# Opening stage in a fixed block order, operands padded to 512 bytes, and 512-column units in the output and last down projections

## The chip, the cores and the metric

The kernel runs on one core of one Trainium2 chip. A core has TensorE (matrix products; PE in the profile, PEld for its weight loads), VectorE (DVE), ScalarE (ACT), GpSimd (POOL) and SyncE (SP, which here only issues DMAs). Each engine works through its own instructions in the order of the program and waits on semaphores for the others. The metric is the device time of one launch in microseconds.

## The reference

A trunk of two layers (`DEPTH = 2`) over 512 latent and 256 context tokens of width 1024, all in fp32. Cut to what matters here:

```
shift, scale, gate  = ada_w, ada_b applied to c (latent) or c_ctx (context)   # per layer
h  = modulate(rms_norm(x), shift, scale)
p  = h @ w_in                       # q, k, v, gMLP, conv and gate columns
m  = gated sum of attention(p) @ w_attn_o, gMLP(p) @ w_gmlp_o, conv(p) @ w_conv_o
x  = x + gate * rms_norm(m @ w_out)                    # output projection
h2 = modulate(rms_norm(x), ...)
x  = x + gate * rms_norm(relu(h2 @ w_ff1) ** 2 @ w_ff2)  # w_ff2: down projection, 4096 -> 1024
```

Layer 0 works on all 768 tokens, layer 1 (the last) on the 512 latent tokens, since only those are put out.

## The kernel before, in words

**Three products for one.** Each operand of a large matrix product is split into a high part that TensorE reads at its fast fp32 rate and the remainder. ScalarE casts the high part (`hi`), VectorE or GpSimd subtracts it (`lo`), and TensorE adds hi·hi, hi·lo and lo·hi into the same sums. `wload` (L165 to L175) does this for a 512 KB block of weights: a DMA into `wraw` or `xraw`, the cast to `whi` (L171), the subtraction to `wlo` (L174). `hT` and `hB` are the split activations, stored with the features on the partitions; `split` (L178, L179) makes them.

**Stages.** A start stage (load and normalise the tokens, compute shift and scale of layer 0), then for each layer attention, gMLP, convolution and feed-forward. Tokens go in tiles of 128 and in groups of two tiles: (0,2), (2,2) and, in layer 0, the context group (4,2). A scheduler that simulates a timeline fixes each engine's order; the code order of the Python text is only its input. Buffers are rings by tag (`whi` and `wlo` four each).

**`natural`** (L460) computes the output projection `w_out` of both layers and the last quarter (`ch == 3`) of the down projection. The activations are the stationary operand, 128 tokens at a time, and the weights stream past in 256 columns, so the 1024 output columns make four units. Unit 0 is done jointly for all groups where `joint` is 1; after that each group runs through its remaining units alone and loads the weights of each unit again. After a unit a `sink` squares and scales the 256 columns, and after a group's last unit `after` runs `post_norm` (sum of squares, reciprocal root, X update at L452) and `pre_norm` (normalise, eight transposes per tile on TensorE at L403, modulate, split) for what follows.

**The opening.** Six token tiles X, the ten small parameter loads, 4 blocks j of shift and scale weights (2 MiB of `ada_w` each, L303, multiplied at L310) and the k and v weights (2 MiB) all come through the DMA queue of SyncE. Normalised tokens are transposed (L403), copied to `xT` (L1066, L1068), modulated when block j's shift and scale are there (L1076), and split into `hT`. `keys_values` in the attention stage (L532) then makes k and v in 144 matmuls of 512 columns, k block by k block over all six token tiles. The q projection follows (L206, 256 columns).

**Where operands lie.** Counted modulo 512 bytes in a partition of the core's memory, the program puts `hT`, `whi` and `wlo` at 256, `hB` at 0, `z` at 64, `attn`, `kT` and `qT` at 320, `gin` at 224.

Of the kernel before, what the change touches and what calls it, by code (L numbers as in the profile page):

```python
# [19 lines left out]
P = 128  # L20
D = 1024
KB = D // P
# [18 lines left out]
JOINT_DOWN = [1, 0]  # L41
# [13 lines left out]
def trunk_kernel(ctx: ExitStack, tc: tile.TileContext, x, c, ctx_in, c_ctx, ada_w, ada_b, mix_pre_g, mix_post_g,  # L55
# [4 lines left out]
    cst = ctx.enter_context(tc.tile_pool(name="cst", bufs=1))  # L60
    outer = ctx.enter_context(tc.tile_pool(name="outer", bufs=1))
# [33 lines left out]

    def o_(shape, tag, bufs, dt=F32):
        return outer.tile(shape, dt, tag=tag, bufs=bufs, name=nm(tag))

    def t_(shape, tag, bufs, dt=F32):
        return stage_pool[0].tile(shape, dt, tag=tag, bufs=bufs, name=nm(tag))  # L100

    ident = cst.tile([P, P], F32, name="ident")
# [8 lines left out]
    for r in range(2):  # L111
        nc.gpsimd.memset(pick[:, r, r:r + 1], 1.0)

# [4 lines left out]
    def here(engine):  # L118

        prev = next((i for i in reversed(nc.cur_bb.bb.instructions) if i.engine == engine), None)  # L120
        if prev is None:
            yield
        else:
            with tc.issue_after(prev):
                yield

# [84 lines left out]
    def wload_kv(l, pool_lo, tiles=range(4)):  # L211
        return [wload(w_in[l][k * 256:(k + 1) * 256, K0:K0 + 512], 2, 512, pool_lo) for k in tiles]

# [42 lines left out]
    def parameters():  # L256
        rows = t_([P, 2, P], "rows", 1)
        nc.sync.dma_start(rows[0:96, 1, :], ada_b.rearrange("l (t p) -> (l t) p", p=P))
        yield
        for i, src in enumerate((mix_pre_g, mix_post_g, gmlp_norm_g, conv_b, conv_norm_g, conv_norm_b,  # L260
                                 ffn_pre_g, ffn_post_g)):
            nc.sync.dma_start(rows[16 * i:16 * i + 16, 0, :], src.rearrange("l (t p) -> (l t) p", p=P))
            if i < 6:
                yield
# [4 lines left out]
        nc.tensor.transpose(pv[:, 0:P], rows[:, 0, :], ident)  # L269
        nc.tensor.transpose(pv[:, P:P + 100], rows[0:100, 1, :], ident[:100, :100])  # L270
# [25 lines left out]
    def ada_shift_scale(j):  # L296
# [10 lines left out]
        for v in range(2):  # L307
            for h in range(2):
                for q in range(4):
                    nc.tensor.matmul(pa[32 * q:32 * q + 32, v * 256:(v + 1) * 256], c2[:, 4 * h + q, :],  # L310
                                     raws[2 * v + h][:, q, :], start=h == 0, stop=h == 1, tile_position=(0, 32 * q))
        rows = t_([P, 512], "adrow", 2)
        nc.scalar.copy(rows, pa)
        pt = ps1()
# [3 lines left out]
        nc.vector.tensor_reduce(m, pt.rearrange("p (v t q s) -> p v t s q", v=2, t=2, q=4)[:, :, :, 0:2, :],  # L318
                                axis=AX.X, op=ALU.add)
        ab = vecs[0]["adab"][:, 0:16].rearrange("p (v k) -> p v k", v=2)[:, :, 2 * j:2 * j + 2]  # L320
        for r in range(2):
            nc.vector.tensor_tensor(m[:, :, :, r], m[:, :, :, r], ab, ALU.add)
        for r in range(2):
            nc.vector.scalar_tensor_tensor(m[:, 1, :, r], m[:, 1, :, r], 1.0, vecs[0]["pre"][:, 2 * j:2 * j + 2],
                                           op0=ALU.add, op1=ALU.mult)
# [74 lines left out]
    def transposed(xn, grp, ps, kb):  # L400
        i0, n, _ = grp
        for i in range(n):
            nc.tensor.transpose(ps[:, i * P:(i + 1) * P], xn[i0 + i][:, kb * P:(kb + 1) * P], ident)  # L403
# [56 lines left out]
    def natural(src, xs, parts, joint, sink, after=None, pool_lo=False):  # L460


        def unit(u, some, after=None):
            ws = wload_n(src[:, u * 256:(u + 1) * 256], pool_lo and u > 2)
            for grp in some:
                i0, n, _ = grp
                ps = ps2()
                for i in range(n):
                    gemm_n(ps[:, i * 256:(i + 1) * 256], (i0 + i) * P, ws, xs)
                sink(grp, u, ps[:, :n * 256].rearrange("p (i c) -> p i c", c=256))  # L470
                if after is not None:
# [790 lines left out]
```

## Time and profile before

| | |
|---|---|
| time, median of 3 runs | 2648.12 us (2647.98 to 2650.31) |
| profiled execution, own time | 2647.3 us |
| its span in the profile | 2645.5 us |
| TensorE busy | 2591.1 us (98%), 15133 matmul records |
| VectorE busy | 1658.5 us (63%) |
| ScalarE busy | 1076.2 us (41%) |
| data moved by DMA | 300.13 MB, mean 113 GB/s |

The span goes from the first to the last instruction; the 1.8 us between it and the execution's own time lie outside. The records of matmuls overlap: one lasts longer than the distance to the next one's start, so what a matmul costs is read from the distance between starts, not from its own duration.

### The profile page before, as it was taken

To read this page: it belongs to the slowest core of one execution; us is meant where nothing else is said; L and a number is where in the kernel's file an instruction comes from. 1 tells how busy PE (TensorE), PEld (TensorE's weight loads), DVE (VectorE), ACT (ScalarE), POOL (GpSimd) and SP (SyncE) were. 2 spreads that over 40 slices of the span, in tenths; PEclk is the share of its full clock that TensorE was granted. 3 is DMA by queue.
4 is the path that set the end of the run, shared out by engine and by line. 5 is a ranking of instruction groups with operands and counts; after the bars stand their busy time and mean duration, and the time that the engine had idled before them with its cause. 6 is when DMAs were issued, how large, how long until landed. Compare 5 with 4: busy or idle time off the path is not lost.

```text
span 2645.5 us, 37736 instructions
## 1 busy us (share of the span) xinstructions
PE 2591.1 (98%) x15133; PEld 2266.0 (86%) x15133; DVE 1658.5 (63%) x2663; ACT 1076.2 (41%) x1848; POOL 435.0 (16%) x310
## 2 busy tenths in 40 slices
PE   7999999999999999999999999999999999999998
PEld 5989988888888899888888899888888888988888
DVE  5746847489864648445564478777679855734436
ACT  4646434344134636322131355554343244633324
POOL 0000015466463200000000000000465510000000
PEclk9999999999999999999999999999999999999999
DMA  7211134233345345243464342112433455533233
GB/s 250 63 43 37 36 107 137 62 99 95 104 130 173 102 165 154 76 130 120 127 199 129 121 151 88 57 41 72 124 108 100 138 159 173 155 112 96 96 101 106
DMA packets 322241, 300.13 MB, mean 113 GB/s; under 512 B 11517, under 2 KB 268817, under 8 KB 322065
## 3 DMA queue, kind: packets, MB, share of 16 engines
q1 hardware_dynamic: 309360, 271.20, 33.2%
q10 hardware_dynamic: 12704, 26.51, 2.8%
q8 instruction: 119, 1.95, 0.3%
q14 instruction: 58, 0.47, 0.1%
HBM read 275.63 MB, written 22.04 MB: 113 GB/s over the span
## 4 chain that ended last, share of the span: by engine, by line
PE 92%; DVE 3%; DMA 2%; ACT 2%; issue 1%; SPq 0%; DVEq 0%; ACTq 0%
PE ps L192 44%; PE ps L494 16%; PE ps L206 9%; PE pq L192 8%; PE pq L206 4%; PE pq L669 3%; PE ps L635 2%; PE ps L658 1%; PE ps L532 1%; DVE wlo L174 1%; ACT whi L171 1%; PE ps L919 1%; PE pq L403 0%; PE ps L574 0%; DMA xraw<-in_ada_w_dram 0%
## 5 line engine op out<-in xcount | busy, mean ns | idle before, releaser
L192 PE MATMUL ps<-hB,whi 128*128 128x512 f32 (+1 forms) x2272 | 591.9, 359 | 5.0 <-DVE ff L1175 2.3
L171 ACT CAST whi<-wraw 128x1024 fp32r<-128x1024 f32 x261 | 273.8, 1050 | 638.8 <-PE ps L192 315.9
L174 POOL TENSOR_TENSOR wlo<-wraw,whi 128x1024 fp32r<-128x1024 f32 x96 | 230.7, 2404 | 1549.2 <-ACT whi L171 1533.5
L192 PEld LDWEIGHTS ps<-hB,whi 128*128 128x128 f32 x2272 | 387.6, 188 | 71.3 <-DVE ff L1175 2.7
L837 DVE SCALAR_TENSOR_TENSOR cy<-G,cw,cy 128x768 f32<-128x768 f32 (+1 forms) x464 | 404.3, 888 | 11.5
L192 PE MATMUL ps<-hB,wlo 128*128 128x512 f32 (+1 forms) x1136 | 371.9, 357 | 0.0
L494 PE MATMUL ps<-whi,hT 128*128 128x512 f32 x1152 | 356.7, 389 | 0.6 <-ACT whi L171 0.6
L174 DVE TENSOR_TENSOR wlo<-wraw,whi 128x1024 fp32r<-128x1024 f32 x165 | 204.7, 1241 | 201.1 <-ACT whi L171 196.8
L192 PE MATMUL ps<-hT,whi 128*128 128x512 f32 (+1 forms) x1408 | 318.7, 344 | 0.6 <-ACT gu L915 0.6
L494 PEld LDWEIGHTS ps<-whi,hT 128*128 128x128 f32 x1152 | 216.2, 188 | 46.4 <-ACT whi L171 1.1
L192 PEld LDWEIGHTS ps<-hT,whi 128*128 128x128 f32 x1408 | 221.1, 189 | 34.3 <-ACT gu L915 1.1
L174 DVE TENSOR_TENSOR wlo<-xraw,whi 128x1024 fp32r<-128x1024 f32 x109 | 133.3, 1223 | 185.0 <-ACT whi L171 184.5
L206 PE MATMUL ps<-whi,hT 128*128 128x256 f32 x1280 | 232.0, 283 | 0.0
L192 PEld LDWEIGHTS ps<-hB,wlo 128*128 128x128 f32 x1136 | 199.4, 188 | 31.6
L494 PE MATMUL ps<-wlo,hT 128*128 128x512 f32 x576 | 224.4, 390 | 0.0
L171 ACT CAST whi<-xraw 128x1024 fp32r<-128x1024 f32 x109 | 114.2, 1049 | 258.9 <-PE ps L494 118.9
L206 PEld LDWEIGHTS ps<-whi,hT 128*128 128x128 f32 x1280 | 199.6, 192 | 0.5 <-issue 0.4
L192 PE MATMUL ps<-hT,wlo 128*128 128x512 f32 x704 | 190.2, 343 | 0.0
L206 PE MATMUL ps<-wlo,hT 128*128 128x256 f32 x640 | 181.2, 284 | 0.6 <-DVE wlo L174 0.6
L343 POOL TENSOR_TENSOR asum<-asum,aprod 128x512 f32<-128x512 f32 x84 | 111.6, 1329 | 105.7 <-ACT aprod L341 63.2
L494 PEld LDWEIGHTS ps<-wlo,hT 128*128 128x128 f32 x576 | 108.1, 188 | 22.6 <-issue 0.4
L192 PEld LDWEIGHTS ps<-hT,wlo 128*128 128x128 f32 x704 | 110.2, 189 | 16.0
(299 smaller groups left out, 4315.1 us busy)
## 6 DMA issues: line engine op xcount, KB each, us to landing
wraw<-in_w_in_dram SPq DMA_DIRECT2D x134, 512.0 KB, 3.7
xraw<-in_w_ff_dram SPq DMA_DIRECT2D x89, 512.0 KB, 3.9
wraw<-in_w_ff_dram SPq DMA_DIRECT2D x63, 512.0 KB, 3.9
xraw<-in_ada_w_dram SPq DMA_DIRECT2D x39, 512.0 KB, 5.2
wraw<-in_ada_w_dram SPq DMA_DIRECT2D x33, 512.0 KB, 4.2
araw<-in_ada_w_dram SPq DMA_DIRECT2D x48, 256.0 KB, 2.9
xraw<-in_w_out_dram SPq DMA_DIRECT2D x18, 512.0 KB, 8.3
wraw<-in_w_attn_o_dram SPq DMA_DIRECT2D x16, 512.0 KB, 3.5
```

The costliest lines, as they stand in the source:

```text
L171: nc.scalar.copy(hi, raw)
L174: e.tensor_tensor(lo, raw, hi.bitcast(F32), ALU.subtract)
L192: nc.tensor.matmul(ps[:, d0:d0 + n], wt[:, k, c0:c0 + P], xt[:, s0:s0 + n], start=k == 0 and j == 0, stop=k == nk - 1 and j == 2)
L206: nc.tensor.matmul(o, xt[:, tok0:tok0 + P], wt, start=k == 0 and j == 0, stop=k == nk - 1 and j == 2)
L343: nc.gpsimd.tensor_tensor(sums[r], sums[r], t, ALU.add)
L494: nc.tensor.matmul(o, xt[:, tok], wt[:, k, :], start=kt == k == j == 0, stop=kt == 3 and k == 1 and j == 2)
L532: nc.tensor.matmul(o, xt[:, tok], wt, start=k == 0 and j == 0, stop=k == KB - 1 and j == 2)
L635: nc.tensor.matmul(ps[:, s0 - key0:s0 - key0 + n], a[:, i * P:(i + 1) * P], b[:, s0:s0 + n], start=m == 0, stop=m == 2)
L658: nc.tensor.transpose(pt[:, kt * P:(kt + 1) * P], Pm[:, kt * P:(kt + 1) * P], ident)
L669: nc.tensor.matmul(po[:, :256], a[:, kt0 + kt, vs], b[:, kt, :], start=kt == 0 and m == 0, stop=kt == nkt - 1 and m == 2)
L837: nc.vector.scalar_tensor_tensor(done if t == TAPS - 1 else y, G[:, :, t:t + 256], cw[:, t * 8 + cidx:t * 8 + cidx + 1], y, op0=ALU.mult, ...
L919: nc.tensor.matmul(ps[:, n * P:(n + 1) * P], gv[cidx // 4][:, n, (cidx % 4) * P:(cidx % 4 + 1) * P], wsT[:, g, :], start=True, stop=True)
```

## The change: what it does

1. **`natural` in two units.** The four units of 256 columns become two of 512, each over all groups; four weight blocks of 256 rows by 512 columns per unit. The output and last down projections together go from 1920 matmuls of 256 columns to 960 of 512, and from 70 weight blocks to 32. Sinks work on 512 columns, and `after` of every group comes in unit 1.
2. **The opening in a fixed order.** X tiles first, then `ada_w` and k/v weights block by block; the k and v matmuls move into the start stage (new L1109), interleaved with the blocks, and TensorE's instructions there are kept in the order in which they are written. The four transposes and the reduction behind each shift and scale block become four matmuls with two moving columns (new L342) and two VectorE operations. The bias load goes to ScalarE's queue, and `xraw` has ten buffers instead of six there.
3. **Padding.** Tiles of 512 bytes or more are padded to multiples of 512, smaller ones go to a pool `tiny`. In the program all operands of matmuls then lie at the same place modulo 512 bytes, 192. Three tags are merged or cut (`gb`, `junkg`, and `dg` from `NT` buffers to 2).

```diff
 def natural(...)
-            ws = wload_n(src[:, u * 256:(u + 1) * 256], pool_lo and u > 2)
-            for grp in some:
...
-                    gemm_n(ps[:, i * 256:(i + 1) * 256], (i0 + i) * P, ws, xs)
...
-        for u in range(joint):
-            unit(u, [grp for part in parts for grp in part])
-        for part in parts:
-            for u in range(joint, 4):
-                unit(u, part, after if u == 3 else None)
+        for u in range(2):
+            ws = [wload(src[kt * 256:(kt + 1) * 256, u * 512:(u + 1) * 512], 2, 512, pool_lo and u == 1)
+                  for kt in range(4)]
+            for grp in groups:
+                i0, n, _ = grp
+                ps = ps2()
+                for k in range(KB):
+                    xhi, xlo = xs[k]
+                    whi, wlo = (w[:, k % 2, :] for w in ws[k // 2])
+                    for i in range(n):
+                        tok = slice((i0 + i) * P, (i0 + i + 1) * P)
+                        for j, (xt, wt) in enumerate(((xhi, whi), (xhi, wlo), (xlo, whi))):
+                            nc.tensor.matmul(ps[:, i * 512:(i + 1) * 512], xt[:, tok], wt,
+                                             start=k == 0 and j == 0, stop=k == KB - 1 and j == 2)
+                sink(grp, u, ps[:, :n * 512].rearrange("p (i c) -> p i c", c=512))
+                if u == 1:
+                    after(grp)
             pump(1)
```

```diff
+    def tile_in(pool, shape, tag, bufs, dt, align=LINE):
+
+        size = 2 if dt == BF16 else 4
+        n = math.prod(shape[1:])
+        whole = -(-n * size // align) * align // size
+        if whole == n:
+            return pool.tile(shape, dt, tag=tag, bufs=bufs, name=nm(tag))
+        t = pool.tile([shape[0], whole], dt, tag=tag, bufs=bufs, name=nm(tag))[:, :n]
...
+    nc.gpsimd.memset(tiny.tile([P, FILL], F32, name="fill"), 0.0)
...
         for t in range(4):
-            nc.tensor.transpose(pt[:, t * P:(t + 1) * P], rows[:, t * P:(t + 1) * P], ident)
+            pe(nc.tensor.matmul(pt[:, 2 * t:2 * t + 2], rows[:, t * P:(t + 1) * P], every, start=True, stop=True))
...
-                dg = t_([P, P], "dg", NT)
+                dg = t_([P, P], "dg", 2)
...
+        in_order[0] = True
...
         for j in range(4):
+            ks = (2 * j, 2 * j + 1)
             if j < 3:
                 next(ada[j + 1])
-            next(ada[j])
-            for grp in (LAT, CTXG):
-                for k in (2 * j, 2 * j + 1):
-                    modulated(grp, k)
+                raws.append(kv_raw(j + 1))
+            w_kv.append(kv_parts(raws[j]))
+            for k in ks:
+                modulated(LAT, k)
+            if j:
+                for k in ks:
+                    modulated(CTXG, k)
+            kv_step(LAT, ks[0])
...
+            if j:
+                kv_step(CTXG, ks[0])
+            kv_step(CTXG, ks[1])
+        in_order[0] = False
```

ScalarE's order in the opening, before. `CAST whi` are the weight casts of k/v blocks, `COPY adrow` takes a block's shift and scale out of the sums, `CAST hT` makes the high part of a feature block of the activations.

```order
L313 COPY adrow_344<-pq_327 128x512
L171 CAST whi_252<-xraw_250 128x1024
L171 CAST whi_258<-xraw_256 128x1024
L1068 COPY xT_78_294<-ps_285 128x256
L178 CAST hT_112<-xT_53_207 128x512
L178 CAST hT_114<-xT_54_209 128x512
...
L313 COPY adrow_393<-pq_376 128x512
L178 CAST hT_116<-xT_56_220 128x512
```

The last two k/v weight casts (`whi_252`, `whi_258`) stand ahead of the first `hT` cast. After the change ScalarE has, from the third k/v block's cast (`whi_540`) on:

```order
L206 CAST whi_540<-xraw_450 128x1024
L206 CAST hT_119<-xT_87_367 128x256
L1081 COPY xT_93_385<-pq_380 128x256
L206 CAST hT_121<-xT_88_369 128x256
L1081 COPY xT_96_394<-pq_389 128x256
L338 COPY adrow_421<-pq_404 128x512
L206 CAST whi_618<-xraw_538 128x1024
L206 CAST hT_123<-xT_58_240 128x512
L206 CAST hT_125<-xT_59_242 128x512
```

`whi_618`, the cast of the fourth and last k/v block, now stands between block 1's shift and scale (`adrow_421`) and block 1's first activations (`hT_123`).

TensorE's order at the end of layer 1's output projection, before: `ps_21197` is the last unit of the second group, 48 matmuls, and `Y_20615`, `Y_20616` are the first group's normalised tiles, transposed for the feed-forward.

```order
L206 MATMUL ps_21197<-whi_21193,hT_20481 128x256
L403 MATMUL pq_20999<-ident,Y_20615 128x128
L403 MATMUL pq_21012<-ident,Y_20615 128x128
L206 MATMUL ps_21197<-wlo_21195,hT_20481 128x256
L206 MATMUL ps_21197<-whi_21193,hT_20482 128x256
```

Two of the sixteen transposes of the first feature blocks stand among the unit's last matmuls. And after the change, where `ps_20141` is the second group's second unit:

```order
L497 MATMUL ps_20141<-wlo_20001,hT_19798 128x512
L497 MATMUL ps_20141<-whi_19999,hT_19799 128x512
L426 MATMUL pq_20089<-ident,Y_19815 128x128
L426 MATMUL pq_20102<-ident,Y_19815 128x128
L426 MATMUL pq_20089<-ident,Y_19816 128x128
L426 MATMUL pq_20089<-ident,Y_19815 128x128
```

The first group's transposes stood behind 133 matmuls of the second group (two whole units and 37 of the third's 48); now they stand behind 48, all of its second unit.

## Rows read from the trace of the kernel before

**Rows 1.** The page: busy time of the engines, and the span in 40 slices (tenths)

```profile
PE 2591.1 (98%) x15133; PEld 2266.0 (86%) x15133; DVE 1658.5 (63%) x2663; ACT 1076.2 (41%) x1848; POOL 435.0 (16%) x310
...
PE   7999999999999999999999999999999999999998
...
PEclk9999999999999999999999999999999999999999
```

**Rows 2.** Chain that ended last, runs of matmuls: start us, us, what

```profile
70.45 17.27 PE pq L206 x144
...
635.60 83.67 PE ps L192 x480
...
825.65 41.61 PE ps L192 x240
...
887.73 67.75 PE ps L192 x384
...
2173.13 56.47 PE ps L192 x247
...
2373.50 43.52 PE ps L192 x192
```

**Rows 3.** TensorE's matmuls by line and shape: busy us, mean ns | idle before

```profile
L206 PE MATMUL ps<-whi,hT 128*128 128x256 f32 x1280 | 232.0, 283 | 0.0
...
L206 PE MATMUL ps<-wlo,hT 128*128 128x256 f32 x640 | 181.2, 284 | 0.6 <-DVE wlo L174 0.6
...
L961 PE MATMUL ps<-dg,means 128*128 128x128 f32 x20 | 2.7, 274 | 0.0
```

**Rows 4.** Windows: stretch, us, busy us of each engine, PEclk, DMA share, GB/s

```profile
20.00:30.00 10.00, 7.77 (x79) 4.27 (x78) 9.39 (x28) 5.09 (x8) 0.00 (x0) 1.00 1.08 391
30.00:40.00 10.00, 9.74 (x56) 7.04 (x54) 3.54 (x9) 2.46 (x7) 0.00 (x0) 1.00 1.09 382
40.00:45.00 5.00, 4.95 (x46) 3.19 (x45) 4.11 (x13) 2.23 (x5) 0.00 (x0) 1.00 0.60 172
...
615.00:635.00 20.00, 14.71 (x85) 12.31 (x85) 17.51 (x23) 10.24 (x13) 14.33 (x13) 0.83 0.28 89
```

**Rows 5.** Timeline of the opening: start us, us, engine, line, operation [idle before]

```profile
23.18 0.69 DVE L1066 COPY xT<-ps 128x512 f32<-128x512 f32 x1
...
25.87 1.05 ACT L171 CAST whi<-xraw 128x1024 fp32r<-128x1024 f32 x1 [0.17 <-DMA xraw<-in_w_in_dram]
...
28.04 0.62 ACT L178 CAST hT<-xT 128x512 fp32r<-128x512 f32 x1 [0.85 <-DVE xT L1076]
...
28.71 0.50 PE L532 MATMUL ps<-whi,hT 128*128 128x512 f32 x1 [0.73 <-ACT hT L178]
...
40.08 1.93 PE L310 MATMUL pq<-xraw,c 128*32 128x256 f32 x32
...
70.29 0.28 PE L206 MATMUL pq<-whi,hT 128*128 128x256 f32 x1
```

**Rows 6.** Chain: 48 matmuls before and 48 after an idle stretch

```profile
581.15 8.33 PE ps L192 x48
...
624.21 10.04 PE ps L192 x48
```

**Rows 7.** Timeline, end of layer 1's output projection, group 0's chain

```profile
2259.36 0.38 ACT L1145 ACTIVATE junk<-ps 128x256 bf16<-128x256 f32 x1 [0.45 <-PE ps L206]
...
2271.60 1.41 DVE L398 TENSOR_SCALAR Y<-X,rs 128x1024 f32<-128x1024 f32 x2
...
2275.06 0.38 PE L403 MATMUL pq<-ident,Y 128*128 128x128 f32 x2
```

**Rows 8.** Timeline, layer 0's last down projection, and the kernel's end

```profile
1597.68 0.41 PE L403 MATMUL pq<-ident,Y 128*128 128x128 f32 x2 [1.15 <-DVE Y L398]
...
2636.89 0.28 PE L206 MATMUL ps<-whi,hT 128*128 128x256 f32 x1
...
2638.79 0.63 DVE L1216 TENSOR_TENSOR Y<-Y,Gb 128x256 f32<-128x256 f32 x1 [1.16 <-ACT junk L1145]
```

More of the change, by code (lines that the diff above doesn't have):

```diff
@@ L40 @@
 UP_AHEAD = 6
-JOINT_DOWN = [1, 0]
+LINE = 512
+FILL = 24
 EPS = 1e-6
@@ L498, in streamed, with attention @@
                 tick(kt)
-    def attention(l, hT, T, last, md, w_kv=None):
+    def attention(l, hT, T, last, md, kv_ps=None):
         NT = T // P
@@ L520, in rope_tabs, with keys_values @@
             return C, S
-        def keys_values(ws):
-            pss = [ps2() for _ in range(3)]
-            for k in range(KB):
-                xhi, xlo = hT[k]
-                whi, wlo = (w[:, k % 2, :] for w in ws[k // 2])
-                for i in range(6):
-                    o = pss[i // 2][:, (i % 2) * 512:(i % 2) * 512 + 512]
-                    tok = slice(i * P, (i + 1) * P)
-                    for j, (xt, wt) in enumerate(((xhi, whi), (xhi, wlo), (xlo, whi))):
-                        nc.tensor.matmul(o, xt[:, tok], wt, start=k == 0 and j == 0, stop=k == KB - 1 and j == 2)
+        def keys_values(pss):
             k_nat = t_([P, 6, 256], "PT", 4)
@@ L1043, in x_load @@
             queue.dma_start(t, src)
-    with stage("start", 6):
+    with stage("start", 10):
         conditioning()
@@ L1051, in trunk_kernel, with x_columns @@
         xT = {}
[L1053 to L1055 removed]
+        def x_columns(grp, kbs):
             w = grp[1] * P
[L1057 to L1059 removed]
+            new, per = (ps2, 1024 // w) if grp == LAT else (ps1, 512 // w)
+            for kb in range(kbs[0], kbs[1], per):
+                ps = new()
                 for q in range(per):
@@ new lines, in kv_step @@
+        def kv_step(grp, k):
+            xhi, xlo = hT[k]
+            whi, wlo = (w[:, k % 2, :] for w in w_kv[k // 2])
+            for i in range(grp[0], grp[0] + grp[1]):
+                o = kv_ps[i // 2][:, (i % 2) * 512:(i % 2) * 512 + 512]
+                tok = slice(i * P, (i + 1) * P)
+                for n, (xt, wt) in enumerate(((xhi, whi), (xhi, wlo), (xlo, whi))):
+                    pe(nc.tensor.matmul(o, xt[:, tok], wt, start=k == 0 and n == 0, stop=k == KB - 1 and n == 2))
+        next(small)
@@ L1083, in trunk_kernel @@
+        x_load(0, X[0:4], 0, nc.sync)
+        ada = [ada_shift_scale(j) for j in range(4)]
+        next(ada[0])
+        next(small)
+        raws = [kv_raw(0)]
+        x_load(0, X[4:6], 4, nc.sync)
+        in_order[0] = True
+        for i in (0, 2):
+            normed(X, xn, (i, 2, 0))
+        next(ada[0])
+        x_columns(LAT, (0, 4))
         for _ in small:
             pass
-        w_kv = wload_kv(0, False, (0, 1))
-        ada = [ada_shift_scale(j) for j in range(4)]
         next(ada[0])
-        x_columns(LAT)
@@ L1164, in trunk_kernel @@
                 nc.scalar.activation(root[:, 0:1], eps, AF.Sqrt)
-            natural(w_out[l], mh, [[g] for g in groups], 1, sink, after)
+            natural(w_out[l], mh, groups, sink, after)
             Y = [t_([P, D], "Y", NT) for _ in range(NT)]
```

121 lines of the change are left out of this document (71 added, 50 removed).

## Prediction

> **What bounds the kernel now.** I read the page first: TensorE is busy 98% of the span, at the full granted clock in every slice, and no other engine is above 63% [rows 1]. So the time is the number of matmuls times their distance, plus the few stretches in which TensorE waits; a transfer or a cast counts only where TensorE ends up behind it. Next I read the chain that ended last, for the distance between starts. A matmul of 512 columns takes 43.52 / 192 = 226.7 ns, one of 256 takes 17.27 / 144 = 119.9 ns, both at the full clock of 2.4 GHz [rows 2]. Columns alone would be 213.3 and 106.7 ns, so each matmul carries about 13.3 ns that don't depend on its width. In layer 0 products over 768 tokens go in pairs, 512 and 256 columns; the sum of both is 346.7 ns, and the chain has pairs at 346.8 (240 matmuls in 41.61), 348.6 (480 in 83.67) and 352.9 (384 in 67.75). Lone matmuls on `z` stand at 228.6 (247 in 56.47) [rows 2]. What these differ in is the place of their operands. Last I read the opening, in windows and on the timeline, and the stage ends.
>
> **Fewer, wider matmuls.** The grouped lines show 1280 + 640 = 1920 matmuls of 256 columns at L206 on `hT` tiles in `ps` [rows 3]: 576 for each of the two products in layer 0 (six token tiles, four units, 24 matmuls each) and 384 in layer 1. Before: 1920 x 120.0 = 230.4 us. After: 960 x 226.7 = 217.6. **-12.8 us.** All of it lies on TensorE, which bounds these stages. Bounds: at the paces of the slowest rows, 228.6 for the new ones, it is -11.0; with 119.9 and 226.7 exactly, -12.6. The Trainium skill (TensorE: Matmul & The Clock Gate, Back-to-back issue gap) gives a lone matmul N/2.4 plus 2.5 ns. By that rule merging two would save 2.5 ns, 960 times, 2.4 us (an estimate from that page), and the forecast would be some 10 us higher; here the rows show 13.3 ns, so they decide.
>
> The 38 weight blocks fewer (70 to 32), each a cast of 1.05 us like the one at 25.87 [rows 5] and a subtraction beside it, take some 40 us off ScalarE and as much off VectorE. Neither is on the path in these stages, so I count nothing for it; if that cover were gone, leaving them out would be a gain, not a loss.
>
> **Opening.** Before, the first k/v matmul starts at 28.71 and the q projection at 70.29 [rows 5], though 144 matmuls at 226.7 ns are only 32.6 us: the other 9 us are waits for, and matmuls of, the blocks of shift and scale. X, `ada_w` and k/v weights are 3 + 8 + 2 MiB = 13.6 MB, and the windows show the queue full at 382 to 391 GB/s until 40 us, then 172 [rows 4]. At 385 that is 35.4 us of transfer after a start of 3 to 4 us, so the last block lands at about 39.5 before and after; no order changes that. What changes is what waits for it. The fourth k/v block comes last, and its cast `whi_618` now stands on ScalarE ahead of `hT_123`, block 1's first activations. Behind that cast are queued the `hT` casts of blocks 1 to 3, and TensorE, in fixed order, waits for them with 108 of the 144 matmuls left. Landing 39.5 + cast 1.05 + `hT` cast 0.62 and the modulation around it [rows 5] puts block 1's first matmul at about 42. Then 108 x 0.2267 = 24.5 us, two blocks of shift and scale matmuls at 1.93 (the row at 40.08), 3.9 together, and some 1.4 for small ones and hand-overs: 71.8, against 70.29: **+1.5**. Bounds: if the block lands early enough that the wait is gone, TensorE runs through from about 24 on and is held by block 3 alone, ending near 65.8: -4.5. If the idle 38 to 42 also lowers the clock, the nearest rows are the stretch 615 to 635, where the granted clock is 0.83 after an idle stretch [rows 4], and 48 matmuls behind it, 10.04 us against 8.33 [rows 6]: +1.7 more, so +3.2; with a later landing, +4.
>
> **Stage ends.** In `natural` the chain of group 0 (squares, root, X update, normalise) must be done when its transposes come up. In layer 1's output projection it took from 2259.36 to 2271.60 + 1.41 = 2273.0, 13.7 us, and the transposes came at 2275.06, so 2.0 us to spare [rows 7]. The cover was 133 matmuls of 0.120, 16 us; it becomes 48 of 0.2267, 10.9 us. The 512-wide square and product make the chain some 0.5 longer, so TensorE is short by up to 14.2 - 10.9 = 3.3 us. Against this stand VectorE and ScalarE, which have no weight blocks of later units to work on in between, so it may be 0. I take the middle, 1.7, for the output projection of either layer: +3.4. In layer 0's last down projection the attention's transposes already wait 1.15 us [rows 8]; its last group's second unit lasts longer than the last unit before, so I take this wait off: -1.15. Together **+2.3** (0 to +6, with each end of the three at its worst).
>
> **Kernel's end.** After the last matmul at 2636.89 the add, the square and the product run on 512 instead of 256 columns. Widths: 0.38 for a 256-column square [rows 7], 0.62 for a 512-column cast on ScalarE, 0.69 for 512 columns on VectorE [rows 5], against 0.63 for the product here [rows 8]. Three operations by 0.1 to 0.27: **+0.7** (0.3 to 0.8).
>
> **`dg` in two buffers.** 20 matmuls of this kind, 0.27 us each [rows 3]; VectorE may now have to wait for the matmul two back. Bounds 0 (VectorE is the slower one) and 20 x 0.1 = 2: **+0.5**.
>
> **Padding.** All operands lie at 192 modulo 512 after the change. If pairs cost 346.7 throughout, the 1968 pairs of the program gain between 1968 x 1.9 = 3.7 us and 1968 x 6.2 = 12.2 us, by the rows at 348.6 and 352.9. If the place has nothing to do with it, 0. No row shows an operand at 192, so I take less than the smaller gain: **-3** (0 to -12.2; the loss is a rival). The Trainium skill (SBUF — State Buffer, Who interferes with whom) gives TensorE two independent read ports, one for moving operands and one for weights, that nobody shares. By that page the place is worth nothing and the forecast 3 us higher; the rows at 346.8 to 352.9 for like work speak for some effect.
>
> The small loads' move to ScalarE's queue and the two-column matmuls are in the opening's sum. **Sum**, against the profiled execution's own 2647.3 (span 2645.5 and 1.8 outside; the median of the runs shown is 0.8 above it): 2647.3 - 12.8 + 1.5 + 2.3 + 0.7 + 0.5 - 3.0 = **2636.5 us**.
>
> **Rivals.** (a) *Padding costs.* If 192 behaves like `z` at 64, which takes 228.6 instead of 226.7, then some 7900 matmuls of 512 columns (5900 lone, 1968 in pairs) lose 1.9 ns: +15 us, and the 3 us of gain fall away: 2636.5 + 18 = 2654.5, slower. It decides from 1.8 ns on, where 2653.4 is reached. For it: `z` is the one place neither at 0 nor 256 for which a lone pace is in these rows. Against it: what differs there is also the distance between the operand and its weights, which is now 0 everywhere. (b) *The 13.3 ns fall with the padding.* Then about 13,900 matmuls gain up to 11 ns or so: -150, 2485. Against it: `hB` lies at a multiple of 512 already, and none of these rows has a matmul below 226.7 or 119.9. (c) *Opening and pairs both at their good end*: -4.5 instead of +1.5 and -12.2 instead of -3: 2621. (d) *The gain goes into waits*: stage ends at +6, opening at +4, `dg` at +2 and the padding at 0: 2636.5 + 3.7 + 2.5 + 1.5 + 3.0 = 2647.2, the same as before.
>
> **How the numbers follow.** A measurement tells 0.2%, 5.3 us, from no change: faster ends at 2642.8, slower begins at 2653.4. The forecast, 2629 to 2643 with its terms between their bounds: 52%. (c) and what lies between: 12%. (b): 8%. (d) and what lies near it: 18%. (a): 10%. Faster 0.72, the same 0.18, slower 0.10. The range leaves out (b) and a little of (a): 2616 (all good ends together, 2618) to 2655.
>
> **What would show it.** Fewer matmuls: L497 in 960 rows, 226.7 ns apart. Opening: TensorE idle at about 38 to 42, ScalarE's cast of the last k/v block ended by its DMA, q at 71.8; right through from 24 says the bound was wrong. Stage ends: waits of 0 to 3 us before the transposes at L426 in both output projections. Padding: pair sums of 346.7 for all operands; 228 or more for lone 512s is rival (a). The forecast is wrong if the chain shows any pace below 226 or above 228, or waits above 10 us in all that the trace before doesn't have.

## The result, and the profile after

The changed kernel takes **2663.51 us** (median of 4 runs, 2661.93 to 2666.47), the kernel before beside it 2649.22 (4 runs, 2647.98 to 2651.86). The ratio is 1.0053, with a 95% interval of 1.0037 to 1.0069: slower by 14.3 us, where 2636.5 was forecast. The profiled execution took 2662.88 us, its span is 2661.1, 15.6 more than before.

The page after, busy times and slices, against [rows 1]:

```profile
PE 2595.8 (98%) x14189; PEld 2223.7 (84%) x14189; DVE 1616.3 (61%) x2566; ACT 1031.7 (39%) x1730; POOL 435.9 (16%) x311
...
PEclk8999999999999999999999999999999999999999
```

TensorE has 944 records fewer, as meant, and VectorE and ScalarE have less to do. Yet TensorE is busy 4.7 us longer. In these slices only the first shows a clock that is no longer full; finer windows below show more such places. Next the chain that ended last (start us, us, what), against [rows 2]:

```profile
85.21 17.27 PE pq L234 x144
...
650.80 83.21 PE ps L220 x480
735.01 84.99 PE ps L220 x480
...
916.61 55.93 PE ps L220 x320
...
982.35 58.08 PE ps L497 x256
```

A matmul of 256 columns still takes 17.27 / 144 = 119.9 ns. The new 512-column ones (L497) take 58.08 / 256 = 226.9, the forecast pace. Pairs take 346.7 (480 matmuls in 83.21), 354.1 (480 in 84.99), 353.3 (240 in 42.40) and 349.6 (320 in 55.93, on `z`): the same scatter as in [rows 2], now that every operand lies at 192. So the paces in the chain don't explain the time. Where it went is read from the same events in both traces:

| event | before, us | after, us | later by |
|---|---|---|---|
| first matmul of the q projection | 70.29 | 85.05 | 14.8 |
| first score matmul of attention | 97.91 | 111.23 | 13.3 |
| layer 0's output projection begins | 965.16 | 982.19 | 17.0 |
| its feed-forward's 288-matmul run (L494, L517) | 1108.98 | 1126.83 | 17.9 |
| layer 1's run of 144 (L206, L234) | 1630.05 | 1648.45 | 18.4 |
| layer 1's feed-forward's run of 192 (L494, L517) | 2329.98 | 2348.07 | 18.1 |
| end of the span | 2645.5 | 2661.1 | 15.6 |

The opening loses 13.3. Up to the output projection 3.7 more go. In the last four rows the wider matmuls bring 3.8, 3.8, 2.6 and 2.6 (288, 288, 192 and 192 pairs of 256 columns, 13.3 ns each by the forecast's paces), 12.8 in all, but the delay falls by 1.4 only: the four stage ends take back 4.7, 4.3, 2.3 and 0.1, together 11.4.

**The opening**, in the windows of [rows 4] (us, busy us of each engine, PEclk, DMA share, GB/s):

```profile
20.00:30.00 10.00, 4.89 (x22) 4.11 (x22) 8.61 (x26) 6.74 (x13) 0.00 (x0) 0.73 1.07 365
30.00:40.00 10.00, 7.51 (x37) 5.75 (x35) 3.84 (x7) 3.15 (x7) 0.00 (x0) 0.93 1.09 353
40.00:45.00 5.00, 3.60 (x33) 1.66 (x34) 2.01 (x5) 0.67 (x3) 0.00 (x0) 0.66 0.67 200
```

From 20 to 30 TensorE is busy 4.89 us of 10 where it was 7.77, and its granted clock is 0.73 where it was 1.00; from 40 to 45 the clock is 0.66. Its timeline (start us, us, line, operation, idle before and releaser) says what it waits for:

```profile
22.74 1.09 PE L426 MATMUL ps<-ident,xn 128*128 128x128 f32 x8 [2.70 <-DVE xT L1079]
24.41 1.75 PE L342 MATMUL pq<-every,adrow 128*128 128x2 f32 x8 [0.58 <-ACT adrow L338]
27.99 0.79 PE L1109 MATMUL ps<-whi,hT 128*128 128x512 f32 x1 [1.83 <-ACT hT L206]
...
41.40 3.46 PE L333 MATMUL pq<-xraw,c 128*32 128x256 f32 x32 [3.40 <-DVE xT L1079]
...
49.14 0.50 PE L1109 MATMUL ps<-whi,hT 128*128 128x512 f32 x1 [0.28 <-ACT hT L206]
```

Transposes, shift and scale, and the first k/v matmul each wait for a copy or a cast made from what came just before, one behind the other. At 41.40 the 32 shift and scale matmuls start after 3.40 us of idling behind transposes whose copy was late, and take 3.46 us, where before they took 1.93 [rows 5]: mostly at 1.2 GHz instead of 2.4. On SyncE's queue and on ScalarE, and then what the queue waited for from 25 to 45 (us in all, times, longest):

```profile
29.96 11.10 SPq L326 DMA_DIRECT2D xraw<-in_ada_w_dram  x4
42.34 0.37 SPq L1094 DMA_DIRECT2D xraw<-in_w_in_dram  x1
...
47.52 1.05 ACT L206 CAST whi<-xraw 128x1024 fp32r<-128x1024 f32 x1 [2.03 <-DMA xraw<-in_w_in_dram]
...
SPq L326 <- DMA xraw<-in_w_in_dram: 3.7, 1, 3.7
SPq L326 <- DVE hT L207: 2.6, 1, 2.6
```

The last `ada_w` loads hold the queue for 11.1 us. They need raw buffers that a k/v block still uses: a transfer of `w_in` and VectorE's subtraction hold them till 40.70. Only the last k/v block, behind them in the queue, waits for the matmuls at 41.40. It is issued at 42.34 and lands at about 47.5; 39.5 was forecast.

**A stage end**, layer 1's output projection, against [rows 7]: ScalarE's first square of group 0, the last normalise, and TensorE around it, then two windows of it.

```profile
2280.78 0.60 ACT L1208 ACTIVATE junk<-ps 128x512 bf16<-128x512 f32 x1 [8.30 <-PE ps L497]
...
2292.13 1.42 DVE L421 TENSOR_SCALAR Y<-X,rs 128x1024 f32<-128x1024 f32 x2
...
2291.17 0.39 PE L497 MATMUL ps<-whi,hT 128*128 128x512 f32 x1
2292.99 0.41 PE L426 MATMUL pq<-ident,Y 128*128 128x128 f32 x2 [1.42 <-issue]
...
2295.24 1.27 PE L220 MATMUL ps<-hB,whi 128*128 128x256 f32 x3 [0.76 <-ACT hB L450]
```

```profile
2293.00:2297.00 4.00, 3.03 (x14) 2.13 (x15) 4.00 (x8) 3.11 (x9) 0.00 (x0) 0.68 0.83 215
2297.00:2301.00 4.00, 4.00 (x21) 4.00 (x20) 4.00 (x13) 2.50 (x7) 0.00 (x0) 0.50 0.28 84
```

The chain of group 0 starts at 2280.78 and its normalising at 2292.13, 11.35 later; TensorE's last matmul of the stage starts at 2291.17, after 10.4. So the transposes wait 1.42 us ("issue" here is a wait whose last releaser the profile doesn't name). What the forecast did not have is the rest: after these waits of 1.42 and 0.76 the clock is granted at 0.68 and 0.50, so that TensorE, busy all the time from 2297 to 2301, works at 1.2 GHz.

Before, the same end had as much waiting. Here are two of its waits, then one window from inside the output projection to the feed-forward's run of 192, before and after:

```profile
2281.13 0.39 PE L192 MATMUL ps<-hB,whi 128*128 128x256 f32 x1 [0.72 <-DVE hB L428]
...
2290.06 0.50 PE L192 MATMUL ps<-hB,whi 128*128 128x256 f32 x2 [1.48 <-DVE ff L1175]
...
2220.00:2329.98 109.98, 106.22 (x795) 101.31 (x795) 70.57 (x130) 58.39 (x125) 0.00 (x0) 1.00 0.54 175
...
2238.00:2348.07 110.07, 106.42 (x605) 93.73 (x605) 63.18 (x116) 51.90 (x103) 0.00 (x0) 0.97 0.47 150
```

TensorE is not busy for 3.76 us of the first window and 3.65 of the second, but the granted clock is 1.00 in the first and 0.97 in the second. So what this end lost is clock, not idle time. Taken the same way over the table's last four stretches, idle time grew by 1.3 us (layer 0's output projection, clock 1.00 before and 0.98 after) and 2.0 (its feed-forward to layer 1's run of 144), then fell by 0.1 and grew by 0.1: 3.3 in all. The rest of the 11.4 is that TensorE's busy time fell by only 4.6 us in these four stretches, instead of 12.8. Most of it is the clock: an estimate from windows of 5 us (busy time, times what the clock lacks to 1.00) gives 3.0 us more than before in layer 0's output projection, 0.7 behind its down projection and 3.0 here, 6.7 together. The waits of the first two, after (us in all, times, longest):

```profile
PE pq L426 <- DVE Y L421: 2.6, 1, 2.6
...
PE ps L234 <- ACT hB L450: 4.0, 4, 1.4
```

### The profile page after: what moved, and what is told of

Its sections match the earlier page's. It is cut to its first block, busy times and chain, and to the rows that moved or that the text cites. A ratio compares the mean times of both kernels' runs of the same rounds, so it can differ in the third digit from the quotient of the medians.

```text
span 2661.1 us, 35469 instructions
## 1 busy us (share of the span) xinstructions
PE 2595.8 (98%) x14189; PEld 2223.7 (84%) x14189; DVE 1616.3 (61%) x2566; ACT 1031.7 (39%) x1730; POOL 435.9 (16%) x311
## 4 chain that ended last, share of the span: by engine, by line
PE 91%; DVE 3%; ACT 3%; DMA 2%; issue 1%; SPq 0%; DVEq 0%; ACTq 0%
PE ps L220 44%; PE ps L517 16%; PE pq L220 8%; PE ps L497 7%; PE pq L234 4%; PE pq L683 3%; PE ps L649 2%; PE ps L672 1%; PE ps L234 1%; DMA xraw<-in_ada_w_dram 1%; PE ps L1109 1%; ACT whi L199 1%; DVE wlo L202 1%; PE ps L933 1%; DMA xraw<-in_w_in_dram 1%
## 5 line engine op out<-in xcount | busy, mean ns | idle before, releaser
L199 ACT CAST whi<-wraw 128x1024 fp32r<-128x1024 f32 x243 | 255.0, 1050 | 626.9 <-PE ps L220 317.5
L517 PE MATMUL ps<-whi,hT 128*128 128x512 f32 x1152 | 356.8, 389 | 0.6 <-ACT whi L199 0.6
L202 DVE TENSOR_TENSOR wlo<-wraw,whi 128x1024 fp32r<-128x1024 f32 x147 | 184.7, 1257 | 200.9 <-ACT whi L199 197.0
L517 PEld LDWEIGHTS ps<-whi,hT 128*128 128x128 f32 x1152 | 216.2, 188 | 46.3 <-ACT whi L199 1.1
L517 PE MATMUL ps<-wlo,hT 128*128 128x512 f32 x576 | 224.4, 390 | 0.0
L202 DVE TENSOR_TENSOR wlo<-xraw,whi 128x1024 fp32r<-128x1024 f32 x85 | 103.9, 1224 | 175.3 <-ACT whi L199 175.1
L497 PE MATMUL ps<-whi,hT 128*128 128x512 f32 x640 | 198.7, 390 | 0.0
L199 ACT CAST whi<-xraw 128x1024 fp32r<-128x1024 f32 x85 | 89.4, 1052 | 238.3 <-PE ps L517 119.0
L497 PEld LDWEIGHTS ps<-whi,hT 128*128 128x128 f32 x640 | 120.1, 188 | 25.1 <-issue 0.4
L517 PEld LDWEIGHTS ps<-wlo,hT 128*128 128x128 f32 x576 | 108.1, 188 | 22.7 <-issue 0.4
L497 PE MATMUL ps<-wlo,hT 128*128 128x512 f32 x320 | 124.5, 391 | 0.0
```

The lines of the kernel that those rows point to most:

```text
L199: nc.scalar.copy(hi, raw)
L202: e.tensor_tensor(lo, raw, hi.bitcast(F32), ALU.subtract)
L497: nc.tensor.matmul(ps[:, i * 512:(i + 1) * 512], xt[:, tok], wt, start=k == 0 and j == 0, stop=k == KB - 1 and j == 2)
L517: nc.tensor.matmul(o, xt[:, tok], wt[:, k, :], start=kt == k == j == 0, stop=kt == 3 and k == 1 and j == 2)
```

## The experiments

Each ratio is to the kernel before, run beside it, with its 95% interval. The delays in us are differences of the medians of the same comparison.

### Units alone, padding alone, both

*e1* has only the first part of the change (the first diff above), *e3* only the third, *e4* both:

```diff
-            natural(w_out[l], mh, [[g] for g in groups], 1, sink, after)
+            natural(w_out[l], mh, groups, sink, after)
```

```diff
-        return outer.tile(shape, dt, tag=tag, bufs=bufs, name=nm(tag))
+        return tile_in(outer, shape, tag, bufs, dt)
...
-                dg = t_([P, P], "dg", NT)
+                dg = t_([P, P], "dg", 2)
```

> The kernel before with only the units of 512 columns in the output and last down projections; opening and padding as before. Theory (the extra time of the change is the opening, +14.8 us, and the units give 12.8 us back of which the stage ends eat about 11): 2647 to 2649 us, the same as before or 1 to 2 us less, with waits of 2 to 3 us before the transposes at the end of both output projections and the first q matmul at 70.3 us as before. Rival (the units gain what was forecast and the loss at the stage ends comes from the padding or the opening): 2636 to 2639 us.

> The kernel before with only the padding, the pool of small tiles and the merged tags. Theory (the place of the operands moves the pair sums of some operands up and of others down, +0.8 us in all by the trace of the changed kernel): 2648 to 2651 us. Rival (padding gains the 3 us forecast or more and something else in the changed kernel hides it): 2646 us or less.

> The changed kernel with the opening of before: units of 512 columns and padding stay. Theory (the opening costs 14.8 us and nothing else in the change depends on it): 2663.5 - 14.8 = 2648.7, between 2647 and 2651 us. Rival (the rest of the change costs as well without it, for instance because the padding slows the q projection): above 2653 us.

Measured: e1 2643.97 us, 0.9982 [0.9973, 0.9991], a gain of 4.3. e3 2653.53, 1.0021 [1.0012, 1.0030], a loss of 5.3. e4 2651.26, 1.0006 [0.9998, 1.0015], a loss of 3.0. So the wider units gain, but a third of 12.8; the padding costs; and the opening makes the difference between e4's 3.0 and the whole change's 14.3, about 11. The parts (-4.3, +5.3, +11.3) add up to 12.3 of the 14.3: e4 is 2.0 worse than e1 and e3 together, which is within the intervals. Of the expectations, e1 ended between its theory and its rival, e3 above its theory's range, and e4 just above its own.

### Giving a stage end its cover back

If the units lose at the stage ends because less work covers group 0's chain, two edits should mend it. *e2* lets each group run both units before the next (the weights are loaded again for each), *e5* takes the units over single tiles, so that a chain is shorter (both on e1):

```diff
-        for u in range(2):
+        for part in parts:
+            for u in range(2):
...
-            for grp in groups:
+                for grp in part:
```

```diff
+            tiles = [(i, 1, g[2]) for g in groups for i in range(g[0], g[0] + g[1])]
-            natural(w_out[l], mh, groups, sink, after)
+            natural(w_out[l], mh, tiles, sink, after)
```

> The kernel before with units of 512 columns, but in the output projections and in layer 0's last down projection each token group runs through both units before the next group starts, with its weights loaded again, so that a group's chain is covered by 96 (layer 0 and 1) matmuls of the next group, 21.8 us, instead of 48, 10.9 us. Theory (the stage ends lose because the cover became shorter than the chain of about 14 us): the waits before the transposes go and the gain of the merge shows, 2636 to 2640 us. Rival (the chain is longer for another reason, such as 512-column sinks or casts in the way, or the merge itself gains less): no more than 3 us below the kernel with joint units.

> The kernel before with units of 512 columns over single token tiles instead of pairs, in the output projections and in layer 0's last down projection: a tile's 24 matmuls run through before the next tile's, so its squares, X update and normalising start 5.4 us before those of the pair's second tile; the transposes stay in pairs, weights are loaded once per unit. Theory (TensorE waits at the stage ends because a chain of 13 us stands against a cover of 10.9): the chain of a single tile is 3 to 4 us shorter, the waits of some 9 us over three stage ends fall to 3 or less, 2637 to 2640 us. Rival (the loss comes with the wide units themselves, as the reloaded weights showed, or from the clock): 2643 us or more, like the kernel with pairs.

Measured: e2 2661.97, 1.0047 [1.0035, 1.0060]; e5 2655.76, 1.0024 [1.0014, 1.0034]. Both lose against e1's gain. TensorE's waits (us in all, times, longest), of e2 and then of e5:

```profile
PE ps L475 <- ACT whi L171: 13.0, 3, 6.5
```

```profile
PE ps L475 <- ACT whi L171: 5.5, 2, 3.7
```

Both times are the rivals', yet neither run tells the theory from its rival, because each makes a new wait. A 512-column unit holds all four `whi` and `wlo` buffers, so the next unit's casts can't begin before its last products let a buffer go, and TensorE waits for them: three times in e2, 13.0 us, and twice in e5, 5.5. More such buffers were not tried.

### Moving the chain itself

*e9* (on e1) gives the subtractions of the first up-projection weights, which stand between the chain's operations on VectorE, to GpSimd; *e12* (on e1) puts these casts and subtractions behind the normalising:

```diff
-                    return wload(w_ff1[l, :, col:col + P], KB, P)
+                    return wload(w_ff1[l, :, col:col + P], KB, P, ch == 0 and j < UP_AHEAD)
```

```diff
-            nc.scalar.copy(hi, raw)
+            with tc.issue_after(behind[0]) if behind else nullcontext():
+                nc.scalar.copy(hi, raw)
...
-            e.tensor_tensor(lo, raw, hi.bitcast(F32), ALU.subtract)
+            with tc.issue_after(behind[1]) if behind else nullcontext():
+                e.tensor_tensor(lo, raw, hi.bitcast(F32), ALU.subtract)
```

> The kernel before with only the units of 512 columns, as in the first experiment, and the subtractions of the first six up-projection weight blocks behind each output projection go to GpSimd, which is idle there. In the trace of the first experiment three of them (1.22 us each on VectorE) stand inside the chain of 13 us that TensorE waits for at the end of the output projection of layer 1. Theory (the wait is chain minus cover, 13.2 against 10.9): the chain gets 3 us shorter, the waits before the transposes at both output projections fall from 2.7 and 1.6 us to under 0.5, and with the waits behind them 2638 to 2642 us. Rival (the wide units lose through something else at the stage ends, or the subtraction at 2.4 us on GpSimd comes too late for the first up matmuls): 2643 us or more.

> The kernel before with only the units of 512 columns, and the casts and subtractions of the first six up-projection weight blocks stand behind the normalising of the group that TensorE waits for, on ScalarE and VectorE, instead of inside its chain. Theory (TensorE waits for chain minus cover: the experiment with GpSimd lengthened the chain to 18.2 us and the wait to 8.5 us): the chain falls from 13.2 to about 10 us, the waits before the transposes of 2.7 and 1.6 us go, 2639 to 2642 us. Rival (the four subtractions, 4.9 us on VectorE, now delay the modulated activations behind the transposes instead, and the wait only moves): 2643 to 2646 us, with new waits before the first up matmuls.

Measured: e9 2653.89, 1.0016 [1.0007, 1.0025], so 9.4 worse than e1; e12 2644.54, 0.9983 [0.9974, 0.9992], like e1. Both times are those of the rivals. In e9 the chain became longer, not shorter. Its timeline at the end of layer 1's output projection:

```profile
2271.05 2.40 POOL L174 TENSOR_TENSOR wlo<-xraw,whi 128x1024 fp32r<-128x1024 f32 x1 [124.64 <-ACT whi L171]
...
2271.40 2.07 DVE L148 TENSOR_TENSOR rst<-rst 128x2 f32<-128x2 f32 x1
...
2273.90 4.55 DVE L452 SCALAR_TENSOR_TENSOR X<-Y,rs,X 128x1024 f32<-128x1024 f32 x2
```

A VectorE operation on two columns takes 2.07 us instead of 0.16, until GpSimd's subtraction ends; the X update takes 4.55 instead of 2.48. The chain's first square, its normalising and the transposes:

```profile
2267.26 0.60 ACT L1145 ACTIVATE junk<-ps 128x512 bf16<-128x512 f32 x1 [8.37 <-PE ps L474]
...
2285.53 1.42 DVE L398 TENSOR_SCALAR Y<-X,rs 128x1024 f32<-128x1024 f32 x2
...
2286.39 2.16 PE L403 MATMUL pq<-ident,Y 128*128 128x128 f32 x8 [8.34 <-issue]
```

From square to normalising it takes 18.27 us, 6.9 more than in e1 (2260.59 to 2271.94, 11.35, as in the changed kernel), and the transposes' wait grows from 1.43 in e1 to 8.34, by 6.9 as well. So at this stage end a microsecond of the chain is a microsecond of TensorE's, which is the theory's core. In e12 the chain is shorter and the transposes come without a wait, but:

```profile
2273.45 1.03 PE L408 MATMUL pq<-ident,Y 128*128 128x128 f32 x8
2276.66 0.80 PE L197 MATMUL ps<-hB,whi 128*128 128x256 f32 x2 [2.17 <-ACT hB L433]
...
2278.05 1.11 PE L408 MATMUL pq<-ident,Y 128*128 128x128 f32 x4 [0.58 <-DVE hf L430]
```

The next product waits 2.17 us for its activations, whose cast on ScalarE stands behind a postponed weight cast (1.03 us from 2274.24) and a square. The 0.58 behind it is VectorE's modulation, late behind the postponed subtractions (4.62 us for four, from 2272.91). Both engines have chain, weights and modulation to do in the same few us; the order among them moves the wait and doesn't remove it: 2.75 us in these two, against some 2.6 in e1 between the same instructions.

### What of the padding costs

*e11* is the kernel before with one number changed:

```diff
-                dg = t_([P, P], "dg", NT)
+                dg = t_([P, P], "dg", 2)
```

> The kernel before with one line changed: dg has two buffers instead of NT. Theory (part of what the padding kernel loses is the wait of 1.3 us before z in the convolution, since VectorE must wait for the matmul two back): 2649 to 2651 us, the wait before the first z matmuls in the trace. Rival (the wait came from the padding): 2648 to 2649 us and no such wait.

Measured: 2652.18, 1.0012 [1.0003, 1.0021], a loss of 3.4. TensorE's timeline of before has the twelve matmuls together; that of e11 follows:

```profile
876.91 1.50 PE L961 MATMUL ps<-dg,means 128*128 128x128 f32 x12
```

```profile
876.94 0.60 PE L961 MATMUL ps<-dg,means 128*128 128x128 f32 x4
...
880.85 0.61 PE L961 MATMUL ps<-dg,means 128*128 128x128 f32 x4
...
884.77 0.61 PE L961 MATMUL ps<-dg,means 128*128 128x128 f32 x4
...
899.69 1.49 PE L192 MATMUL ps<-z,whi 128*128 128x512 f32 x5 [1.31 <-ACT z L178]
```

With two buffers TensorE takes four at a time with other matmuls of its order between them, and VectorE waits for a buffer meanwhile. The last sum ends 7.0 us later (885.38 against 878.41). The first matmul on `z` comes in time, at 896.12 against 896.09, but a later block of `z`, which hangs on these sums, makes TensorE wait 1.31 us at 899.69, where it ran without a wait before. That is less than half of the 3.4 (0.8 to 5.6 by the interval); no run tells where the rest is. By the medians the two `dg` buffers are the larger part of the padding's 5.3. e3 has the same wait (1.3 us at `z`) and its q projection 1.9 us later, but e4, which is padded too, has q at 70.4 as before; the rest is spread in pieces that no run here tells apart.

### The opening

*e6* takes the last k/v casts and subtractions out of the way of the activations, *e7* also moves the ten small parameter loads to GpSimd's queue, *e8* also issues each k/v block ahead of the `ada_w` block; *e10* leaves TensorE's order to the scheduler. All are the whole change; e6 has the first of these edits, e7 the first two (the second for all ten loads), e8 all three, and e10 only the last:

```diff
-            w_kv.append(kv_parts(raws[j]))
+            with here(ACT_E), here(DVE_E):
+                w_kv.append(kv_parts(raws[j]))
...
-        nc.sync.dma_start(rows[96:98, 1, :], q_norm_g)
+        nc.gpsimd.dma_start(rows[96:98, 1, :], q_norm_g)
...
-                next(ada[j + 1])
                 raws.append(kv_raw(j + 1))
+                next(ada[j + 1])
```

```diff
-        in_order[0] = True
```

> The changed kernel, but each k/v block's cast and subtraction may not stand ahead of what its engine does for the blocks before. Theory (a cast that waits for its transfer holds up the copies of the context tiles behind it, these hold TensorE's shift and scale matmuls of block 1, and these hold the raw buffers that the last transfers need): the wait of 3.4 us before block 1's shift and scale matmuls goes, the last k/v block lands some 3 to 4 us earlier, q starts at 76 to 80 instead of 85.1, 2655 to 2659 us. Rival (the transfers are late by themselves, through the ten small loads ahead of them): q not before 83, 2661 us or more.

> As the kernel with the later casts, and the ten small parameter loads are issued by GpSimd instead of SyncE, where they stood ahead of the k/v weights from 6.5 to 15.8 us. Theory (both hold up the transfers): the gap in the transfers at 13 to 17 us goes, everything behind it comes 3 to 4 us earlier, q at 72 to 76, 2651 to 2655 us. Rival (with the casts out of the way the small loads hide beside other work): within 1 us of the kernel with the later casts alone.

> As the kernel before this one, and each k/v block is loaded ahead of the shift and scale weights of its block instead of behind them, so that the last k/v block doesn't need a raw buffer that block 1's shift and scale matmuls release. Theory (that buffer is the last thing that delays it): q 1 to 3 us earlier still, at 70 to 74, 2649 to 2653 us. Rival (the last shift and scale block, now last in the queue, takes its place): no change to 1 us.

> The changed kernel with TensorE's order in the opening left to the scheduler instead of the written order. Theory now (the written order leaves TensorE idle while block 0's shift and scale go through copy, modulation and split, from 19.7 to 28 us, and again at each block, and the clock falls behind these idle stretches; late transfers are second): the k/v and q matmuls end some 8 to 12 us earlier, 2652 to 2656 us. Rival (the block-by-block transfers and dependencies set the time whatever the order on TensorE): 2661 us or more.

Measured: e6 2664.91, 1.0062 [1.0049, 1.0075]; e7 2663.80, 1.0057 [1.0045, 1.0069]; e8 2664.27, 1.0059 [1.0044, 1.0074]: nothing gained by any beyond its interval (e8's runs scatter from 2658.0 to 2670.4, and its trace is of the fastest). e10 2654.49, 1.0022 [1.0013, 1.0031]: a loss of 5.7 instead of 14.3, as its theory had it. My second theory, that late transfers and casts hold the opening, fell by the times, though what it named did move. In e6 the wait of 3.4 us is gone and the first q matmul stands at 74.29; in e8 it stands at 73.20. But the last k/v matmul comes at 86.06 in e6 and 83.56 in e8 (84.83 in the changed kernel), because block 3's activations now stand on VectorE behind subtractions of the next product's weights (2.35 us for two in e6, at 69.68), and the first score matmul comes at 114.36 and 111.38 instead of 111.23. In e8 the last k/v block is issued at 25.82 instead of 42.34, and its first window is no better:

```profile
20.00:30.00 10.00, 3.66 (x20) 3.13 (x19) 8.40 (x24) 3.85 (x8) 0.00 (x0) 0.74 1.09 353
```

The order is what costs. The windows of e10, and two lines of its timeline; then one window from 20 to 70, of before, the changed kernel and e10:

```profile
20.00:30.00 10.00, 7.39 (x24) 5.93 (x25) 8.96 (x25) 6.15 (x12) 0.00 (x0) 0.66 1.08 366
30.00:40.00 10.00, 9.40 (x74) 6.61 (x73) 4.97 (x10) 4.08 (x9) 0.00 (x0) 1.00 1.08 353
...
24.58 0.79 PE L1109 MATMUL ps<-whi,hT 128*128 128x512 f32 x1 [0.22 <-ACT hT L206]
...
36.58 1.93 PE L333 MATMUL pq<-xraw,c 128*32 128x256 f32 x32
```

```profile
20.00:70.00 50.00, 47.47 (x316) 34.47 (x316) 32.99 (x106) 19.17 (x37) 0.00 (x0) 1.00 0.68 227
...
20.00:70.00 50.00, 38.39 (x230) 26.87 (x230) 25.56 (x59) 18.08 (x33) 0.00 (x0) 0.86 0.68 221
...
20.00:70.00 50.00, 45.57 (x273) 34.12 (x274) 30.99 (x71) 20.46 (x38) 0.00 (x0) 0.90 0.72 228
```

The first k/v matmul starts 3.4 us earlier, the block of 32 at 36.58 instead of 41.40 and at full clock, though its last k/v cast comes at 45.32, hardly earlier than 47.52. The scheduler puts k/v matmuls, and later the q projection's, where TensorE would wait. So 14.3 - 5.7 = 8.6 of the opening's 11.3 are the written order, and 2.7 what else changed in the opening (a difference of medians, with a few us of noise; and a scheduler that is free on TensorE also places the other engines' work anew). From 20 to 70 TensorE stands idle for 2.5 us before, 11.6 in the changed kernel and 4.4 in e10. So most of the 8.6 is idle time, 7.2; the clock, 0.86 against 0.90, is the smaller part.

## Why the prediction was wrong

**Fewer, wider matmuls: right.** -12.8 forecast, and the 512-column matmuls took 226.9 ns, after as in e1 (58.05 for 256). The fixed 13.3 ns of a matmul is saved, as the rows said.

**Opening: the step that failed first.** "TensorE, in fixed order, waits for them with 108 of the 144 matmuls left", one wait from 38 to 42, was the whole of it: +1.5, with +4 at the worst. Measured: some 11 by the experiments, 13.3 by the events. The cast of the last k/v block did stand where the forecast saw it, but three terms failed. The landing at 39.5 took the queue as full to the end; the `ada_w` loads waited for raw buffers that a k/v block still used, the last block came at 47.5, and block 1's first k/v matmul at 49.14 instead of 42. From there to q the forecast had 29.8 us (24.5 + 3.9 + 1.4), and 35.9 went by: the hand-overs, put at 1.4 with the small matmuls, are waits again at blocks 2 and 3, since in fixed order the matmul that could fill such a wait stands behind the one that waits. And the lower clock was priced at one place only, while the granted clock is 0.73, 0.93 and 0.66 in the three windows above. From 20 to 70 that makes 9.1 us more idle time than before and, as an estimate, 38.39 x 0.14 = 5.4 us of clock, for a q that comes 14.8 later. e6 to e8 show that the late block alone is not the cause, and e10 that the order is.

**Stage ends: mis-sized.** Chain against cover was the right mechanism (e9), and in layer 1's output projection the wait was as forecast: 1.42 us, where 1.7 was taken. But the sum of three ends was +2.3, at most +6; the events say +11.3, and e1 alone, 12.8 - 4.3, says 8.5. The waits were not far off in sum: TensorE's idle time grew by 3.3 us, if not where it was forecast. Layer 0's output projection waits longer (2.58 at the transposes), and after its down projection, where a wait of 1.15 was to fall away, the first products of layer 1's attention (L234) wait for the modulated `hB`. The term that was missing is the clock, which the forecast priced in the opening and put at nothing here without a reason: of the other 8.2 us some 6.7 are a lower clock by the estimate above, and the last 1.5 no run here divides. Layer 1's end is the plain case: it cost 2.3 us more than before with no more idle time. Why the chip grants less clock after than before, with as much waiting, no run tells.

**Kernel's end.** +0.7 forecast; 2.6 gained by the matmuls and 2.5 by the delay leave +0.1.

**`dg`.** +0.5 forecast, 0 to 2; e11 measured +3.4. The bound looked at 20 matmuls' own waits and not at what stands between them in TensorE's order; 1.31 us of the loss is traced.

**Padding.** -3 forecast, measured 0 in sum on the paces: pairs at 346.7 to 354.1 ns with all operands at 192 show that the place alone doesn't explain the scatter of [rows 2]. One pace did move. The last 111 lone matmuls on `z` before layer 1's output projection took 25.41 us before, from 2204.02 to 2229.43, 228.9 ns each, and as much in e1, which isn't padded; after, 25.16 us, 226.7 each, as in e3 and e4, which are:

```profile
2222.65 0.62 PE L220 MATMUL ps<-z,whi 128*128 128x512 f32 x2
...
2247.81 0.39 PE L497 MATMUL ps<-whi,hT 128*128 128x512 f32 x1
```

Pairs on `z` fell from 352.9 to 349.6, while the pairs of the run of 480 at 735.01 stand at 354.1, above all of [rows 2]. Whether it is the place of `z` or its distance from the weights, no run tells. Rival (a), 1.9 ns more per matmul, is wrong by the same rows: `z` at 192 takes 226.7, and the new lone ones 226.9. (The row of 228.6 that the prediction gives to `z` begins with matmuls on `hB`; its `z` part alone is 228.9.) The padding kernel is slower all the same, by other ways (`dg`). The Trainium skill (SBUF — State Buffer, Who interferes with whom) gives TensorE's moving operands and weights a read port each that nobody shares. It names no price for a place there; the lone pace of `hB` agrees with that (114.26 us for 504 matmuls before, at 0, and after, at 192), and that of `z` doesn't, so here the measurement decides.

**The rivals.** Nearest was (d), the gain goes into waits; its price was 10.7 us above the forecast, and the measured time is 27 above it. The sign was wrong by the opening's landing and hand-overs and by the clock at the stage ends. The sum of (d) also takes +6 for the stage ends, where two ends at 3.3 are 6.6. The condition named, "waits above 10 us in all that the trace before doesn't have", is the one that came true: 9.1 us more idle time from 20 to 70 and 3.3 in the stages behind. The best kernel measured is e1, the wider units alone: 2643.97 us, 4.3 below before; e12 is its equal.

## What to carry to other kernels

Where one engine bounds a kernel, a wait is not priced by its length: look also at the clock granted behind it, at the waits of before in the same place, and at what stands behind the waiting instruction in its order. A written order loses what a scheduler fills in, so compare the two before keeping either. When fewer and larger units replace many small ones, check the buffers that a unit holds and the work that covers the chain between two stages, and bound a smaller ring of buffers by what stands between its users, not by their own durations.

## What the runs showed of the hardware

GpSimd held VectorE up fully: a VectorE operation on two columns, 0.16 us elsewhere, took 2.07 us beside a GpSimd subtraction of 2.40 (e9), and ended only as that ended; the subtraction kept its length. The Trainium skill (SBUF — State Buffer, Who interferes with whom) says that these two share a pair of ports, taken by one of them as a whole; e9 agrees, and shows that an operation of two columns pays as much as a large one: 1.91 us more, against 2.07 more for two X updates of 1024 columns.

TensorE's clock fell to 1.2 GHz after idle stretches as short as these: 1.42 and 0.76 us close together at the end of layer 1's output projection were followed by 0.68 and 0.50 in two stretches of 4 us, while 32 matmuls in the opening took 3.46 us instead of 1.93. But before, waits of 0.72 and 1.48 us, 8.9 us apart at the same end, left it at 1.00. So the length of the waits alone doesn't tell what the clock does; what else counts, no run here shows.

Matmuls of 512 columns on `z` took 228.9 ns apart with `z` at 64 modulo 512 bytes and the weights at 256, and 226.7 with both at 192 (25.41 and 25.16 us for 111); those on `hB` took 226.7 at 0 as at 192. Why, no run here tells.
